# A decoder trunk's routing stage: PSUM operands for the choice of experts, three tiles chosen at once, and a new order of the first rows

## Chip, cores and metric

One core of one Trainium2 chip runs the whole kernel. The metric is device microseconds (us) of one execution; several executions are timed and the median is taken. Engines are named as in the profile: PE (matmuls), DVE, ACT, POOL, and SP, which issues the weight loads.

## What is computed

Two layers, 512 tokens of width 1024, everything in float32. Each layer is a mixer (attention of several kinds), an output projection with a layer norm, a router that sends every token to two of 16 experts, and the experts.

```python
x = layer_norm(ALPHA * x + mixer(x) @ w_o)             # "the output projection"
aff = sigmoid(x @ router_w)                            # 16 experts in 4 groups
sel = aff + router_bias
# group score: sum of the two highest sel of a group; the best group is kept,
# and in it the two highest experts; their aff, divided by their sum, are the gates
x = layer_norm(ALPHA * x + sum_e gate_e * (silu(x @ wg_e) * (x @ wu_e)) @ wd_e)
```

## The kernel before

**Tiles.** The residual `xr` lies in SBUF as four tiles of 128 tokens, two to a buffer (tiles 0 and 1 in "pair 0", tiles 2 and 3 in "pair 1"). A product in float32 is three matmuls (`mm3`): the operand is split into a high part (a cast on ACT, L185) and a low part (a subtraction on DVE, L186), and high by high, high by low and low by high are summed in PSUM (L198 to L200).

**Output projection and routing** (`out_proj`). For each tile and each half of 512 columns PE makes 12 matmuls, DVE adds the result to `xr` (L571) and takes statistics, PE transposes the sum (L576) and multiplies it by the router's weights (L580). With the statistics complete a Newton root on DVE gives the deviation, a sigmoid on ACT the affinities, ACT normalises the tile (L589), and `affine` applies the norm's gain and bias as two tensor operations, by POOL, for the last tile in part by DVE (L255, L256). Then POOL stores the tile twice to DRAM (`x1d`, L591, from which the experts' rows are gathered, and `yd`, L594, to which they are added). `choose` (L413 on) finds the two experts of each token, `slots` gives each token a slot of 96 in its expert, and `first_rows` (L490) multiplies `xr` by a one-hot matrix and so collects the first expert's rows without a gather. These three run for tiles 0 and 1, then tile 2, then tile 3 (`ROUTE_ORDER`).

**Experts** (`moe`). For every expert there are six loads of 1 MB: gate, up and down in two halves each, 96 a layer, all issued by SP in one order and each into a buffer of one of several kinds. The letter string `slot_of` gives the kind for each load in turn; "0" and "1" are the two pairs of `xr`, free as soon as their last reader, the stores among them, is done. The first 16 loads (`AHEAD`) are issued during the mixer and the output projection. `load` takes a ready one from a dictionary, and what isn't there it fetches:

```python
def load(w, e, c):
    if (w, e, c) in ahead:
        return ahead.pop((w, e, c))
    k = nload[0]
    nload[0] += 1
    return fetch(slot_of[k], w, e, c)
```

The order of PE for the first expert is: the gate's product ("g0", eight blocks k0 to k7 of three matmuls, two blocks to a half of a load), the up product ("u0"), the transposes of the next expert's rows (`rows_in(1)`, L1111), then the gate's product of expert 1 ("g1"). `put_rows` copies the first rows from PSUM as high and low part (L203, L204). `after_slots` (L493 to L529) makes one-hot matrices of the slots on DVE and multiplies them on PE, once into the token index of each slot (`idx`, L507, by which POOL gathers the rows of experts 1, 2 and so on, L1100), once into the gate of each slot (`gslot`). It is written before the first expert; the scheduler of the framework places its small matmuls between those of g0. The scheduler orders each engine's instructions by the order in the program and by what is ready in its own estimate; `tc.issue_after(x)` forces what is written inside it to stand behind `x` on the same engine.

Of the kernel before, what the change touches and what calls it, by code (L numbers as in the profile page):

```python
# [54 lines left out]
ROUTE_ORDER = "y0 l0 y1 l1 y2 l2 y3 l3 r02 r23 r34"  # L55
# [12 lines left out]
def trunk_kernel(ctx: ExitStack, tc, x_in, even_w_in, even_b_f, even_sinks, odd_w_in,  # L68
# [92 lines left out]
    hold = [None]  # L161
    in_order = [False]
# [25 lines left out]

    def ksplit(w, n, eng=V):
# [5 lines left out]
        return rows  # L195

    def mm3(o, lh, ll, rh, rl, first, last):
        T.matmul(o, lh, rh, start=first, stop=False)  # L198
        T.matmul(o, lh, rl, start=False, stop=False)  # L199
        T.matmul(o, ll, rh, start=False, stop=last)  # L200

    def split_to(hdst, ldst, src):
        first(A.copy(hdst, src))  # L203
        first(V.tensor_tensor(out=ldst, in0=src, in1=hdst.bitcast(F32), op=ALU.subtract))  # L204

    def rsqrt(var, eps, n, pin=lambda ins: ins):
# [20 lines left out]
        c = square(q, v)  # L227
        pin(V.scalar_tensor_tensor(out=p, in0=c, scalar=-10.0 / 3, in1=c, op0=ALU.add, op1=ALU.mult))
# [184 lines left out]
    def choose(t0, t1):  # L413

        n = t1 - t0
        ts_ = slice(t0, t1)
        sel = sm.tile([128, NT, NE], F32, name="sel", bufs=1)[:, 0:n]
        V.tensor_tensor(out=sel, in0=aff[:, ts_], in1=rb.unsqueeze(1).to_broadcast([128, n, NE]), op=ALU.add)
        sg = sel.rearrange("p t (g j) -> p (t g) j", j=4)
# [3 lines left out]
        V.tensor_tensor(out=pr[:, :, 2:4], in0=sg[:, :, 0:4:2], in1=sg[:, :, 1:4:2], op=ALU.add)  # L423
        V.tensor_tensor(out=pr[:, :, 4:5], in0=sg[:, :, 0:1], in1=sg[:, :, 3:4], op=ALU.add)
        V.tensor_tensor(out=pr[:, :, 5:6], in0=sg[:, :, 1:2], in1=sg[:, :, 2:3], op=ALU.add)
        gs = sm.tile([128, NT, 4], F32, name="gs")[:, 0:n]
        V.tensor_reduce(out=gs.rearrange("p t g -> p (t g)"), in_=pr, axis=AX.X, op=ALU.max)
# [22 lines left out]
        f8 = sm.tile([128, NT, 2], F32, name="rf8")[:, 0:n]  # L450
# [3 lines left out]
        V.tensor_tensor(out=M[:, ts_], in0=O[:, ts_, 0, :], in1=O[:, ts_, 1, :], op=ALU.add)  # L454
# [12 lines left out]
    def slots(sl, oh0, t0, t1):  # L467
# [5 lines left out]
        for j in range(1, t1):  # L473
# [5 lines left out]
        return V.tensor_tensor(out=oh0[:, t0:t1], in0=slot1.unsqueeze(1).to_broadcast([128, n, CAP]),  # L479
                               in1=sl[:, t0:t1, 0:1].to_broadcast([128, n, CAP]), op=ALU.is_equal)  # L480

    def first_rows(ps2, oh0, t0, t1):

        for c in range(2):
# [8 lines left out]
    def after_slots(sl, oht, flag):  # L493

        Of = O.rearrange("p t c e -> p (t c) e")
        R = sm.tile([128, NT * 2, NE], F16, name="R", bufs=1)
        V.tensor_tensor(out=R, in0=Of, in1=recc.rearrange("p t c -> p (t c)").unsqueeze(2).to_broadcast([128, 8, NE]), op=ALU.mult)
# [3 lines left out]
        V.tensor_reduce(out=pos, in_=t.rearrange("p t c e -> p (t c) e"), axis=AX.X, op=ALU.add)  # L501
        sp = ps_s()
        for j in range(NT * 2):
            oh = sm.tile([128, CAP], F16, name="oh", bufs=4)
            V.tensor_scalar(oh, slot1, pos[:, j:j + 1], None, op0=ALU.is_equal)
            T.matmul(sp[:CAP, 0:NE], oh, R[:, j, :], start=(j == 0), stop=(j == NT * 2 - 1))
        V.tensor_scalar(idx[:CAP], sp[:CAP, 0:NE], OOB, None, op0=ALU.add)  # L507
# [11 lines left out]
        weights()  # L519

        og = sm.tile([128, NT * 2, NE], F32, name="og", tag="gt", bufs=1)
        V.tensor_tensor(out=og, in0=O.rearrange("p t c e -> p (t c) e"),
                        in1=gates.rearrange("p t c -> p (t c)").unsqueeze(2).to_broadcast([128, 8, NE]), op=ALU.mult)
        sg = ps_t()
        for j in range(NT * 2):
            eq = sm.tile([128, CAP], F32, name="eq")
            V.tensor_scalar(eq, slot1, pos[:, j:j + 1], None, op0=ALU.is_equal)
            T.matmul(sg[:CAP, 0:NE], eq, og[:, j, :], start=(j == 0), stop=(j == NT * 2 - 1))
        A.activation(out=gslot[:CAP], in_=sg[:CAP, 0:NE], func=AF.Copy, scale=1.0 / ALPHA)  # L529

    def half_proj(chunk, oH, oL, g, i):
        o = ps_a()
        for k in range(4):
            ts_ = slice(i * 128, (i + 1) * 128)
            mm3(o, oH[4 * g + k][:, ts_], oL[4 * g + k][:, ts_], *chunk[k], k == 0, k == 3)
        return o

    def out_proj0(chunk_src, oH, oL, g, cs=range(2)):

        for c in cs:  # L540
            rows = ksplit(wload(chunk_src(c, g), 4, 512), 2, G)
            for i in range(NT):
                ys = xr[i][:, c * 512:(c + 1) * 512]
                V.scalar_tensor_tensor(out=ys, in0=ys, scalar=ALPHA, in1=half_proj(rows, oH, oL, g, i),
                                       op0=ALU.mult, op1=ALU.add)

    def out_proj(l, chunk_src, oH, oL, g, x1d, yd, work, main):
# [5 lines left out]
        sts = [sm.tile([128, 2, 6], F32, name="st", tag="st", bufs=4) for _ in range(NT)]  # L553
        if main:
            rwg, rsc = router_fold(l)
            u = sm.tile([128, NT, NE], F32, name="u", bufs=1)
            lgs = ps_s()[:, 0:2 * NT * NE].rearrange("p (c t e) -> p c t e", c=2, t=NT)
# [3 lines left out]
            work.tile([128, 4, CAP], F32R, name="hH", tag="hH")  # L561
            work.tile([128, 4, CAP], F32R, name="hL", tag="hL")
# [4 lines left out]

        def tile_y(i):
            for c in range(2):
                ys = xr[i][:, c * 512:(c + 1) * 512]  # L570
                V.tensor_tensor(out=ys, in0=ys, in1=half_proj(rows[c], oH, oL, g, i), op=ALU.add)  # L571
                V.bn_stats(sts[i][:, c, :], ys)
                if main:
# [3 lines left out]
                    yT = work.tile([128, 512], F32, name="yT", tag="sg", bufs=2)  # L577
                    A.copy(yT, p)
                    for k in range(4):
                        T.matmul(lgs[:, c, i, :], yT[:, k * 128:(k + 1) * 128], rwg[:, c * 4 + k, :],  # L580
                                 start=(k == 0), stop=(k == 3))

        def tile_ln(i):
            mv, rs = ln_stats(sts[i:i + 1])
# [822 lines left out]
```

## Time and profile before

| what | value |
|---|---|
| time, median of 3 runs | 1175.6 us (1171.33 to 1185.86) |
| the profiled execution | 1180.26 us, of which 1178.5 us are the span of the trace |
| PE busy | 1093.0 us, 93% of the span |
| DVE busy | 934.3 us, 79% |
| ACT busy | 762.3 us, 65% |
| POOL busy | 266.5 us, 23% |
| moved by DMA | 262.25 MB, mean 223 GB/s |

"Busy" is the time in which an engine has an instruction in execution. The profile's granted clock of TensorE is a share of 2.4 GHz: 1.00 is that, 0.50 is 1.2 GHz. A share of DMA near 1 says that the 16 DMA engines always had packets in flight. The routing stage of the first layer lies at some 220 to 288 us of the span, that of the second at 790 to 875 us.

### The profile page before, as it was taken

How to read it: one execution, taken by the hardware profiler on the slowest of the kernel's cores; microseconds unless marked ns; L12 is line 12 of the kernel's file. 1: busy time of each engine (PE TensorE's matmuls, PEld its weight loads, DVE VectorE, ACT ScalarE, POOL GpSimd, SP SyncE). 2: the span in 40 equal slices, each digit the busy share in tenths (PEclk: the TensorE clock that was granted, in tenths of full speed). 3: DMA queues.
4: the chain of work that ended last, by engine and by line, in shares of the span. 5: the costliest groups of instructions: out<-in, count | busy, mean ns of one | idle time of the engine just before them, and what ended most of it. 6: DMA issues, size and time to landing. Idle time of an engine off the chain costs nothing. (4 is left out here: it accounts for less than half of the span.)

```text
span 1178.5 us, 16701 instructions
## 1 busy us (share of the span) xinstructions
PE 1093.0 (93%) x5775; PEld 817.5 (69%) x5775; DVE 934.3 (79%) x1866; ACT 762.3 (65%) x1229; POOL 266.5 (23%) x223
## 2 busy tenths in 40 slices
PE   8999989979999999998599898999799999999982
PEld 7786767867777777776377665777677777777761
DVE  4646756597999999987766998766879999999976
ACT  4556646235888888887435744654268888888862
POOL 2001340251111141112613133003411111411023
PEclk9999999988999999999699998999789999999997
DMA  8314332779999997998512211335699999989972
GB/s 209 117 40 90 75 88 105 255 276 303 302 358 357 350 334 237 361 357 279 183 28 72 73 37 37 107 108 209 240 299 285 365 342 353 339 255 366 371 234 108
DMA packets 139613, 262.25 MB, mean 223 GB/s; under 512 B 11831, under 2 KB 28247, under 8 KB 139520
## 3 DMA queue, kind: packets, MB, share of 16 engines
q1 hardware_dynamic: 129232, 234.62, 57.9%
q0 software_dynamic: 10288, 26.48, 9.1%
q8 instruction: 47, 0.77, 0.3%
q14 instruction: 46, 0.38, 0.1%
HBM read 246.73 MB, written 22.30 MB: 228 GB/s over the span
## 5 line engine op out<-in xcount | busy, mean ns | idle before, releaser
L186 DVE TENSOR_TENSOR wl<-wraw,wh 128x1024 fp32r<-128x1024 f32 (+1 forms) x418 | 503.6, 1231 | 83.3 <-ACT wh L185 74.9
L185 ACT CAST wh<-wraw 128x1024 fp32r<-128x1024 f32 (+3 forms) x436 | 445.7, 1039 | 155.0 <-PE ps_s L200 63.8
L198 PE MATMUL ps_s<-wh,m 128*96 128x512 f32 (+1 forms) x528 | 208.3, 394 | 1.7 <-ACT m L203 1.7
L199 PE MATMUL ps_s<-wl,m 128*96 128x512 f32 (+1 forms) x528 | 206.4, 391 | 0.0
L200 PE MATMUL ps_s<-wh,m 128*96 128x512 f32 (+1 forms) x528 | 205.0, 388 | 0.4 <-DVE m L204 0.4
L200 PEld LDWEIGHTS ps_s<-wh,m 128*96 128x96 f32 x528 | 86.4, 164 | 35.7 <-DVE m L204 1.3
L198 PEld LDWEIGHTS ps_s<-wh,m 128*96 128x96 f32 x528 | 86.7, 164 | 34.8 <-ACT m L203 2.1
L199 PEld LDWEIGHTS ps_s<-wl,m 128*96 128x96 f32 x528 | 86.4, 164 | 31.9 <-issue 0.2
L198 PE MATMUL ps_a<-wh,hH 128*96 128x512 f32 x256 | 102.7, 401 | 3.8 <-ACT hH L203 3.8
L199 PE MATMUL ps_a<-wl,hH 128*96 128x512 f32 x256 | 101.8, 398 | 4.0 <-POOL wl L186 4.0
L200 PE MATMUL ps_a<-wh,hL 128*96 128x512 f32 x256 | 101.0, 394 | 1.3 <-DVE hL L204 1.3
L198 PE MATMUL ps_a<-wh,XH 128*128 128x512 f32 (+2 forms) x224 | 89.4, 399 | 4.3 <-ACT wh L185 3.2
L1100 POOL DMA_INDIRECT m<-x1d,idx x30 | 33.1, 1104 | 255.8 <-PE ps_t L1111 224.2
L200 PE MATMUL ps_a<-wh,XL 128*128 128x512 f32 (+2 forms) x224 | 88.7, 396 | 1.9 <-DVE XL L204 1.9
L1175 POOL DMA_INDIRECT yd<-m,idx x30 | 49.2, 1640 | 177.0 <-ACT m L1174 173.3
L199 PE MATMUL ps_a<-wl,XH 128*128 128x512 f32 (+2 forms) x224 | 88.8, 396 | 0.0
L199 PE MATMUL ps_a<-XL,wh 128*128 128x512 f32 x160 | 65.0, 406 | 0.0
L200 PE MATMUL ps_a<-XH,wl 128*128 128x512 f32 x160 | 64.7, 405 | 0.3 <-DVE wl L186 0.3
L198 PE MATMUL ps_a<-XH,wh 128*128 128x512 f32 x160 | 64.6, 403 | 0.0
L357 ACT ACTIVATE p<-p,nm 128x256 f32<-128x256 f32 (+3 forms) x96 | 50.6, 529 | 17.8 <-DVE nm L350 8.8
L376 ACT COPY pT<-ps_t 128x512 f32<-128x512 f32 (+2 forms) x88 | 43.4, 517 | 28.8 <-PE ps_t L373 28.0
L199 PEld LDWEIGHTS ps_a<-wl,hH 128*96 128x96 f32 x256 | 41.3, 161 | 20.5 <-POOL wl L186 5.4
(327 smaller groups left out, 1918.3 us busy)
## 6 DMA issues: line engine op xcount, KB each, us to landing
wraw<-in_moe_w_up_dram SPq DMA_DIRECT2D x64, 1024.0 KB
wraw<-in_moe_w_gate_dram SPq DMA_DIRECT2D x64, 1024.0 KB
wraw<-in_moe_w_down_dram SPq DMA_DIRECT2D x64, 1024.0 KB
wraw<-in_w_o_dram SPq DMA_DIRECT2D x6, 1024.0 KB
wraw<-in_even_w_in_dram SPq DMA_DIRECT2D x4, 1024.0 KB
x1d<-xr POOLq DMA_DIRECT2D x8, 512.0 KB
yd<-xr POOLq DMA_DIRECT2D x8, 512.0 KB
xr<-yd SPq DMA_DIRECT2D x8, 512.0 KB
```

The costliest lines, as they stand in the source:

```text
L185: first(A.copy(hv, w))
L186: first(eng.tensor_tensor(out=lv, in0=w, in1=hv.bitcast(F32), op=ALU.subtract))
L198: T.matmul(o, lh, rh, start=first, stop=False)
L199: T.matmul(o, lh, rl, start=False, stop=False)
L200: T.matmul(o, ll, rh, start=False, stop=last)
L357: A.activation(out=pt[h], in_=(pt if bias else Sp)[h], func=AF.Exp, bias=nm[:, h:h + 1], scale=(slopes[0][h] if slopes else 1.0), accum_ou ...
L376: A.copy(d_, s_)
L1100: G.indirect_dma_start(out=xg_of[e], out_offset=None, in_=x1d[:, :], in_offset=bass.IndirectOffsetOnAxis(ap=idx[:CAP, e:e + 1], axis=0), b ...
L1175: G.indirect_dma_start(out=yd[:, :], out_offset=bass.IndirectOffsetOnAxis(ap=idx[:CAP, e:e + 1], axis=0), in_=yos[e % 2], in_offset=None, ...
```

## The change

**The choice.** The sigmoid is written twice, to `aff` in SBUF and to spare columns of the PSUM bank that holds the router's logits; in `choose` each operation with two tensors takes one of them from PSUM. The root for one tile uses operations with two scalars from memory in place of a second tensor. Tiles 0, 1 and 2 are chosen at once, then tile 3.

**The norm.** The variance of tiles 0 and 1 comes from a Square on ACT. The affine of tiles 0 to 2 is all on POOL; tile 3's is done in four steps on DVE (`centre` and `whole`, each for two halves).

**The first rows.** The last tile's steps, the first rows' parts and g0's low parts follow each other in a written order (`in_turn`). The token index is made between k5 and k6 of g0 (`between`), the gates of the slots after u0, and what is needed only at the layer's end in expert 4.

**The first gate's weights.** g0's four halves of loads are cut by a comprehension that calls `load` once per half.

```diff
-AHEAD = (2, 3, 4, 0, 1, 5, 6, 8, 9, 10, 12, 13, 7, 14, 11, 15)
-LN1_DVE = (0, 0, 0, 256)
+AHEAD = (2, 3, 4, 0, 1, 5, 6, 8, 9, 10, 12, 13, 14, 11, 15, 7)
-ROUTE_ORDER = "y0 l0 y1 l1 y2 l2 y3 l3 r02 r23 r34"
+ROUTE_ORDER = "y0 l0 y1 l1 y2 l2 c03 y3 s03 l3 r03"
...
-    def choose(t0, t1):
+    def choose(t0, t1, sc):
+        affp, selp, gp, f8 = (t[:, ts_] for t in sc)
-        V.tensor_tensor(out=sel, in0=aff[:, ts_], in1=rb.unsqueeze(1).to_broadcast([128, n, NE]), op=ALU.add)
+        for t in (selp, sel):
+            V.tensor_tensor(out=t, in0=affp, in1=rb.unsqueeze(1).to_broadcast([128, n, NE]), op=ALU.add)
-        V.tensor_tensor(out=pr[:, :, 0:2], in0=sg[:, :, 0:2], in1=sg[:, :, 2:4], op=ALU.add)
+        V.tensor_tensor(out=pr[:, :, 0:2], in0=sg[:, :, 0:2], in1=sp[:, :, 2:4], op=ALU.add)
...
+        def centre(h):
+            return V.scalar_tensor_tensor(out=ys, in0=ys, scalar=end["mu"], in1=gb[:, cs], op0=ALU.subtract, op1=ALU.mult)
+        def whole(h):
+            return V.scalar_tensor_tensor(out=ys, in0=ys, scalar=end["rs"], in1=bb[:, cs], op0=ALU.mult, op1=ALU.add)
...
-        g0 = [ksplit(load("g", 0, c), 2) for c in range(2)]
-        for c in range(2):
-            put_rows(c, ps2[c])
-        after_slots(sl, oht, flag)
-        for e in (1, 2):
-            gather(e)
+        with tc.issue_after(route["act"].ins):
+            raws = [load("g", 0, c)[:, u * 2:u * 2 + 2, :] for c in range(2) for u in range(2)]
+            units = []
+            for w in raws:
+                with tc.issue_after(units[-1][2].ins) if units else nullcontext():
+                    units.append(high(w))
+        in_turn(lambda: route["whole"](0))
+        route["rows"](0)
+        low_part(0)
+        in_turn(lambda: route["whole"](1))
+        route["rows"](1)
+        route["x1"]()
+        in_turn(lambda: put_rows(0, ps2[0]))
+        low_part(1)
+        in_turn(lambda: put_rows(1, ps2[1]))
+        low_part(2)
+        def between():
+            with tc.issue_after(last_mm[0].ins):
+                in_turn(lambda: found.extend(slot_tokens(sl, route["room"])) or found[0])
+            low_part(3)
+            for i in (1, 2):
+                gather(i)
...
         for e in range(NE):
-            g = up("g", e, None if e else g0)
+            g = up("g", e, *((None,) if e else (g0, 1, between)))
+            if e == 4:
+                with tc.issue_after(act_op[0].ins):
+                    for_the_end(sl, oht, flag)
...
             sg = act(g, u, n)
+            if e == 0:
+                with tc.issue_after(put.ins):
+                    slot_weights(found[1])
```

The order of SP's loads around the end of the first layer's output projection, before (the first two rows are the last ahead loads, `wraw50` and `wraw52` are the two pairs of `xr`, and the two loads into them are the gate halves of expert 3):

```order
L1092 DMA wraw4_2822<-in_moe_w_gate_dram 128x4x512 [waits DMAHW0_49]
L1092 DMA wraw_2824<-in_moe_w_down_dram 128x4x512 [waits DMASW5_49,DMASW4_49,DMAHW1_49,DVE_49,Pool_49]
L1092 DMA wraw50_3346<-in_moe_w_gate_dram 128x4x512 [waits DMASW4_49,DMASW5_49,DMASW3_49,DMAHW2_49,DMASW2_49,PE_49]
L1092 DMA wraw52_3368<-in_moe_w_gate_dram 128x4x512 [waits DMASW6_49,DMASW1_49,DMASW7_49,DMASW0_49,DMAHW3_49,PE_49,Activation_49]
L1092 DMA wraw4_3400<-in_moe_w_up_dram 128x4x512 [waits DMAHW4_49,DVE_49]
```

The same place of SP now:

```order
L1196 DMA wraw4_2781<-in_moe_w_gate_dram 128x4x512 [waits DMAHW7_49,DMASW2_49]
L1196 DMA wraw50_2789<-in_moe_w_gate_dram 128x4x512 [waits DMASW3_49,DMASW4_49,DMASW2_49,DMASW5_49,DVE_49,DMAHW0_49,PE_49,Pool_49]
L1196 DMA wraw_2783<-in_moe_w_down_dram 128x4x512 [waits DMAHW1_49,DVE_49,Pool_49]
L1196 DMA wraw50_3662<-in_moe_w_gate_dram 128x4x512 [waits DMAHW2_49,DMAHW0_49,DVE_49]
L1196 DMA wraw3_2785<-in_moe_w_up_dram 128x4x512 [waits DMAHW3_49,DVE_49,Activation_49]
L1196 DMA wraw52_2791<-in_moe_w_gate_dram 128x4x512 [waits DMASW6_49,DMASW7_49,DMASW1_49,DMAHW4_49,DMASW0_49,PE_49]
L1196 DMA wraw52_3684<-in_moe_w_gate_dram 128x4x512 [waits DMAHW5_49,DMAHW4_49,DVE_49]
L1196 DMA wraw4_3310<-in_moe_w_gate_dram 128x4x512 [waits DMAHW6_49,DVE_49]
```

Two more gate loads stand in the row (272 weight loads in the whole program where there were 268), `wraw50_2789` and `wraw52_2791`, both into the pairs of `xr`, both behind waits on stores (DMASW) and on PE. In the second layer the two stand directly one after the other, behind the second down half.

DVE at the first rows of the first layer, now (`wl` is a low part, `m2` the first rows, `xr2` the pair of tiles 2 and 3; L680 is `whole`):

```order
L680 SCALAR_TENSOR_TENSOR xr2_130<-xr2_130,rs_o_2682,lnt_2296 128x512 [waits DMASW3_49]
L195 TENSOR_TENSOR wl_2794<-wraw3_2761,wh_2793 128x1024 [waits DMAHW5_49,Activation_49]
L680 SCALAR_TENSOR_TENSOR xr2_130<-xr2_130,rs_o_2682,lnt_2296 128x512
L214 TENSOR_TENSOR m2_2788<-ps_o_2345,m2_2788 128x384 [waits Activation_49]
L195 TENSOR_TENSOR wl_2797<-wraw50_2789,wh_2796 128x1024 [waits DMAHW0_49,Activation_49]
L214 TENSOR_TENSOR m2_2788<-ps_s_2346,m2_2788 128x384 [waits Activation_49]
L195 TENSOR_TENSOR wl_2800<-wraw3_2763,wh_2799 128x1024 [waits DMAHW6_49]
...
L537 TENSOR_SCALAR idx_135<-ps_s_2849 96x16 [waits PE_49]
L195 TENSOR_TENSOR wl_2803<-wraw52_2791,wh_2802 128x1024 [waits DMAHW4_49,Activation_49]
L186 TENSOR_TENSOR wl_2879<-wraw4_2755,wh_2878 128x1024 [waits DMAHW2_49,Activation_49]
```

The low parts of g0 come from four buffers: the two ahead loads (`wraw3_2761`, `wraw3_2763`) and the two new loads. Before, they came from the two ahead loads alone, and were made before the first rows were there.

PE at the end of u0 in the first layer, now (L546 are the gates of the slots, L1215 the transposes of expert 1's rows, the last row begins g1):

```order
L209 MATMUL ps_s_2877<-wl_2903,m2_2788 96x512
L210 MATMUL ps_s_2877<-wh_2902,m2_2788 96x512
L546 MATMUL ps_t_2931<-og_2929,yT_2850 96x16 [waits DVE_49]
L546 MATMUL ps_t_2931<-og_2929,yT_2850 96x16 x3
L546 MATMUL ps_t_2931<-og_2929,yT_2856 96x16 x4
L1215 MATMUL ps_t_2941<-ident_77,m1_2787 128x96 [waits DMASW2_49]
L1215 MATMUL ps_t_2941<-ident_77,m1_2787 128x96 x3
L1215 MATMUL ps_t_2948<-ident_77,m1_2787 128x96 [waits Activation_49]
L1215 MATMUL ps_t_2948<-ident_77,m1_2787 128x96 x3
L208 MATMUL ps_s_3000<-wh_3001,m2_2788 96x512 [waits Activation_49]
```

And DVE's row up to the `og` that L546 waits for:

```order
L186 TENSOR_TENSOR wl_3002<-wraw4_2759,wh_3001 128x1024 [waits Activation_49]
L488 TENSOR_TENSOR as__2925<-a2_2923 128x4 [waits DVE_49]
L186 TENSOR_TENSOR wl_3006<-wraw4_2759,wh_3005 128x1024 [waits Activation_49]
L489 RECIPROCAL as__2925<-as__2925 128x4 [waits DVE_49]
L186 TENSOR_TENSOR wl_3022<-wraw2_2765,wh_3021 128x1024 [waits DMAHW7_49,Activation_49]
L490 TENSOR_TENSOR gates_134<-a2_2923,as__2925 128x8 [waits DVE_49]
L186 TENSOR_TENSOR wl_3026<-wraw2_2765,wh_3025 128x1024 [waits Activation_49]
L542 TENSOR_TENSOR og_2929<-O_132,gates_134 128x128 [waits DVE_49]
```

The gates' matmuls moved from between those of g0 and u0 to behind u0, and their operand `og` stands on DVE behind the four low parts of g1.

## Rows read from the trace of the kernel before

**Rows 1.** Busy time of each engine in a stretch of the experts: PE, PEld, DVE, ACT, POOL, clock, DMA, GB/s.
```profile
300.00:320.00 20.00, 20.00 (x99) 14.30 (x98) 18.64 (x21) 17.16 (x22) 3.62 (x3) 1.00 0.97 320
```

**Rows 2.** DVE in order of time, first layer; columns: start, duration, engine, line, operation.
```profile
234.30 0.69 DVE L571 TENSOR_TENSOR xr<-xr,ps_a 128x512 f32<-128x512 f32 x1 [0.52 <-PE ps_a L200]
235.64 1.74 DVE L418 TENSOR_TENSOR sel<-aff,rb 128x32 f32<-128x32 f32 x1
237.51 2.40 DVE L423 TENSOR_TENSOR pr<-sel 128x16 f32<-128x16 f32 x1
...
247.97 0.67 DVE L571 TENSOR_TENSOR xr<-xr,ps_a 128x512 f32<-128x512 f32 x1
252.18 0.69 DVE L571 TENSOR_TENSOR xr<-xr,ps_a 128x512 f32<-128x512 f32 x1 [0.48 <-PE ps_s L475]
```

**Rows 3.** POOL in order of time, beside rows 2.
```profile
234.94 2.39 POOL L255 TENSOR_TENSOR xr<-xr,lnt 128x1024 f32<-128x1024 f32 x1 [1.80 <-ACT xr L589]
237.41 2.46 POOL L256 TENSOR_TENSOR xr<-xr,lnt 128x1024 f32<-128x1024 f32 x1
```

**Rows 4.** DVE, first layer: choosing for tile 3, its first and its last operation.
```profile
263.80 0.16 DVE L418 TENSOR_TENSOR sel<-aff,rb 128x16 f32<-128x16 f32 x1
266.42 0.17 DVE L454 TENSOR_TENSOR M<-O 128x16 f16<-128x16 f16 x1
```

**Rows 5.** PE, first layer: transposes that waited for an add, and two matmuls soon after.
```profile
242.58 0.66 PE L576 MATMUL ps_t<-ident,xr 128*128 128x128 f32 x4 [2.90 <-DVE xr L571]
...
247.27 0.63 PE L200 MATMUL ps_a<-wh,XL 128*128 128x512 f32 x1
247.70 0.63 PE L198 MATMUL ps_a<-wh,XH 128*128 128x512 f32 x1
```

**Rows 6.** Busy time of each engine in three windows of the routing stages, columns as in rows 1.
```profile
245.00:250.00 5.00, 5.00 (x16) 4.23 (x17) 3.49 (x7) 2.29 (x3) 1.87 (x1) 0.50 0.13 52
270.00:275.00 5.00, 5.00 (x27) 4.25 (x27) 2.25 (x9) 1.62 (x4) 0.00 (x0) 0.61 0.92 363
...
855.00:860.00 5.00, 4.38 (x28) 4.31 (x25) 2.79 (x14) 0.96 (x2) 0.00 (x0) 0.50 0.91 328
```

**Rows 7.** DVE, second layer: the fifth of the eight adds.
```profile
819.47 0.69 DVE L571 TENSOR_TENSOR xr<-xr,ps_a 128x512 f32<-128x512 f32 x1 [0.52 <-PE ps_a L200]
```

**Rows 8.** PE: the first matmul of g0 and the transposes behind u0, both layers.
```profile
272.57 0.77 PE L198 MATMUL ps_s<-wh,m 128*96 128x512 f32 x1
285.97 0.82 PE L1111 MATMUL ps_t<-ident,m 96*128 96x96 f32 x8
...
859.64 0.77 PE L198 MATMUL ps_s<-wh,m 128*96 128x512 f32 x1
873.18 0.82 PE L1111 MATMUL ps_t<-ident,m 96*128 96x96 f32 x8
```

**Rows 9.** POOL: the first of tile 3's two stores, both layers.
```profile
264.06 0.59 POOL L591 DMA_DIRECT2D x1d<-xr  x1 [0.30 <-POOL xr L256]
851.33 0.59 POOL L591 DMA_DIRECT2D x1d<-xr  x1 [0.82 <-DVE eq L512]
```

**Rows 10.** SP: the two loads into the pairs of `xr` as one group, both layers.
```profile
264.39 10.54 SPq L1092 DMA_DIRECT2D wraw<-in_moe_w_gate_dram  x2
851.46 11.74 SPq L1092 DMA_DIRECT2D wraw<-in_moe_w_gate_dram  x2
```

**Rows 11.** ACT and DVE, first layer: a high and a low part of a weight.
```profile
274.91 1.05 ACT L185 CAST wh<-wraw 128x1024 fp32r<-128x1024 f32 x1 [1.38 <-DMA wraw<-in_moe_w_gate_dram]
276.24 1.22 DVE L186 TENSOR_TENSOR wl<-wraw,wh 128x1024 fp32r<-128x1024 f32 x1
```

**Rows 12.** PE, g0 in the second layer: two matmuls that follow each other without a gap.
```profile
868.16 0.40 PE L199 MATMUL ps_s<-wl,m 128*96 128x512 f32 x1
868.40 0.39 PE L200 MATMUL ps_s<-wh,m 128*96 128x512 f32 x1
```

**Rows 13.** PE, first layer: four of the eight matmuls that make the gates of the slots.
```profile
276.54 0.43 PE L528 MATMUL ps_t<-og,eq 128*96 128x16 f32 x4
```

More of the change, by code (lines that the diff above doesn't have):

```diff
@@ L187, in unit, with high, low @@
         return h, l
+    def high(w):
+        h, l = (hl.tile([128, 1024], F32R, name="w" + t.lower(), tag=t).rearrange("p (a b) -> p a b", a=2) for t in "HL")
+        return h, l, A.copy(h, w)
+    def low(w, h, l):
+        return V.tensor_tensor(out=l, in0=w, in1=h.bitcast(F32), op=ALU.subtract)
     def ksplit(w, n, eng=V):
@@ L453, in choose @@
                         in1=f8.rearrange("p t c -> p (t c)").unsqueeze(2).to_broadcast([128, 2 * n, NE]), op=ALU.is_equal)
-        V.tensor_tensor(out=M[:, ts_], in0=O[:, ts_, 0, :], in1=O[:, ts_, 1, :], op=ALU.add)
+        with nc.allow_low_precision("ones and zeros"):
+            return V.tensor_reduce(out=M[:, ts_], in_=O[:, ts_].rearrange("p t c e -> p t e c"), axis=AX.X, op=ALU.add)
     def weights():
@@ L518, in after_slots, with half_proj @@
         V.tensor_reduce(out=flag, in_=cnt[:, 0:NE], axis=AX.X, op=ALU.max)
[L519 to L531, printed above, removed]
+    def half_proj(chunk, oH, oL, g, i, behind=None):
         o = ps_a()
@@ L534, in half_proj @@
             ts_ = slice(i * 128, (i + 1) * 128)
-            mm3(o, oH[4 * g + k][:, ts_], oL[4 * g + k][:, ts_], *chunk[k], k == 0, k == 3)
+            with tc.issue_after(behind.ins) if behind and k else nullcontext():
+                mm3(o, oH[4 * g + k][:, ts_], oL[4 * g + k][:, ts_], *chunk[k], k == 0, k == 3)
         return o
@@ L566, in out_proj, with room, by_act @@
         rows = [ksplit(wload(chunk_src(c, g), 4, 512), 2) for c in range(2)]
+        def room():
+            return work.tile([128, 512], F32, name="yT", tag="sg", bufs=2)
+        def by_act(i):
+            return main and i < 2
+        sts = [sm.tile([128, 2, 6], F32, name="st", tag="st", bufs=4) for _ in range(NT)]
         def tile_y(i):
@@ L583, in tile_ln @@
+        end = {}
         def tile_ln(i):
-            mv, rs = ln_stats(sts[i:i + 1])
+            if by_act(i):
+                V.tensor_scalar(ls[:, i, 2:3], ls[:, i, 1:2], -1.0 / (D * 32), None, op0=ALU.mult)
+                A.activation(out=sq, in_=xr[i], func=AF.Square, bias=ls[:, i, 2:3], scale=1.0 / 32,
+                             accum_out=ls[:, i, 4:5])
+                rs = rsqrt(ls[:, i, 4:5], LN_EPS, 1)
+            else:
+                mv, rs = ln_stats(sts[i:i + 1])
             if main:
@@ new lines, in tile_ln @@
+                A.activation(out=sc[0][:, i, :], in_=u[:, i, :], func=AF.Sigmoid)
+                end["act"] = A.activation(out=aff[:, i, :], in_=u[:, i, :], func=AF.Sigmoid)
+            if i == NT - 1 or not main:
+                end.update(mu=mv[:, 0, 0:1], rs=rs)
+                return
+            nm = sm.tile([128, 1], F32, name="nmr", bufs=4)
+            if by_act(i):
+                V.tensor_scalar(nm, ls[:, i, 2:3], 32.0, rs, op0=ALU.mult, op1=ALU.mult)
+            else:
+                V.tensor_scalar(nm, mv[:, 0, 0:1], -1.0, rs, op0=ALU.mult, op1=ALU.mult)
@@ L591, in tile_ln, with x1 @@
+            with tc.issue_after(end["act"].ins):
+                A.activation(out=xr[i], in_=xr[i], func=AF.Identity, scale=rs, bias=nm)
+            affine(xr[i], gb, bb, 0)
+            x1(i)
+        def x1(i):
             nc.gpsimd.dma_start(x1d[i * 128:(i + 1) * 128, :], xr[i])
```

187 lines of the change are left out of this document (124 added, 63 removed).

## Prediction

> **What bounds the kernel now.** I read the busy shares first, then the windows, then each engine in order of time in the two routing stages. Inside the experts PE has no gap: 20.00 of 20 us busy at a clock of 1.00 [rows 1], so nothing that the change does there can help, and each matmul added there costs its time. It touches the stages between the output projection and the second expert, where PE waits and then runs slowly. The reader sees it in [rows 5]: the transposes of the sixth add wait 2.90 us, and the matmuls after them follow each other by 0.43 us (247.27 to 247.70), against 0.24 us at full clock [rows 12]. The clock is 0.50 in 245 to 250 and 855 to 860 and 0.61 in 270 to 275 [rows 6], that is at or near 1.2 GHz instead of 2.4. A wait of some 3 us is paid twice, then: as idle time, and in slow matmuls for some 5 us after it.
>
> The wait comes from DVE: adding the router's bias takes 1.74 us and one addition of pairs 2.40 us [rows 2], where the same bias addition takes 0.16 in [rows 4]. Each of the two ends with a POOL affine that began before it or with it (234.94 and 2.39, 237.41 and 2.46) [rows 3]. Both slow operations read two tensors from SBUF; the add of the projection, which reads one from PSUM, takes its usual 0.69 beside the first affine [rows 2].
>
> **Sum, part 1: up to the first matmul of g0.** With one operand in PSUM I take those two operations at 0.16 each, so 3.8 us go. Undisturbed adds follow each other by 4.2 us (247.97 to 252.18) [rows 2]. From the fifth add at 234.30 the seventh then comes at 242.7 instead of 247.97; in the second layer, from 819.47 [rows 7], at 827.9. Call it t. The added operations are short: sigmoid and bias are written twice (four instructions a layer at some 0.2), and choosing three tiles adds six searches at some 0.2, while one call of 2.8 us [rows 4] goes.
>
> What is late next is the eighth add: it stands on DVE behind the choice of tiles 0 to 2. Statistics, root and sigmoid of the third tile are about 3.4 us (an estimate: 0.7 like the add, twelve short operations at 0.2, the sigmoid), the choice of three tiles 4.5 (2.8 for one tile [rows 4] and the longer searches), with a gap 8.4 us instead of 4.2: t+8.4. PE idles some 3 us there, and the clock falls again, as after the 2.90 us of [rows 5]. Then tile 3: transposes, logits and root at half clock 4.6, sigmoid 0.4, first `centre` and choice 3.4, second `centre`, slots and one-hot 1.1, `whole` 0.7 (0.69 for 512 columns [rows 2]), a low part 1.2 [rows 11], `whole` 0.7: t+20.5. The stores of tile 3 are issued at about t+20.6 = 263.3 and 848.5, against 264.06 and 851.33 [rows 9], and g0's first matmul runs at about t+21 = 264 and 849, against 272.57 and 859.64 [rows 8]. That is 8.6 and 10.6 us gained at this point. Most of it is the low parts and the token index that no longer stand ahead of g0.
>
> **Part 2: the weights of g0.** The gain isn't kept, and this is the core of the forecast. The comprehension calls `load` for g0's first half, which pops the ahead load, and then again for the same half, which is no longer in the dictionary: so it is fetched a second time, into the pairs of `xr`. The order shows both: two gate loads more a layer, and their low parts in g0's row. Blocks k2 and k3 use the first reload, k6 and k7 the second. The first goes into pair 0, whose tiles were stored long before. The second goes into pair 1 and needs tile 3's two stores landed. Before, the load into that pair stood under the same condition but was for expert 3, and nobody waited for it. How long it takes is in [rows 10]: SP's group of two ends at 274.93 and 863.20, so with about 0.5 us for the issue the second went out at 274.4 and 862.7, 10.4 and 11.4 us after the store's issue [rows 9], while loads shared the DMA.
>
> First layer: 263.3 + 10.4 = 273.7. Then the reload must land. Alone, 1.05 MB at 363 GB/s (270 to 275 in [rows 6]) are 2.9 us; with the two MB issued just ahead of it 8.7. I take 6.8: 280.5. High and low part are 1.05 and 1.22 [rows 11], so k6 starts at 282.8. Blocks k0 to k5 are over by some 274, so PE has idled long and starts at half clock: of the 30 matmuls left to the end of u0, 14 at 0.43 and 16 at 0.24 are 9.8 us: 292.6, against 285.97 [rows 8], **+6.6 us**.
>
> Second layer: 848.5 + 11.4 = 859.9, here both reloads stand ahead of the next loads, 5 us: 864.9; k6 at 867.2, u0 ends at 877.0, against 873.18 [rows 8]: **+3.8 us**. Bounds of this part: with the reload landing 2.9 us after its issue, 3.9 and 2.1 us less; with all the two MB ahead in the way, and the stores delayed by the 2.9 us of one more MB, 4.8 and 6 more.
>
> **Part 3: gates of the slots behind u0.** L546 waits for `og`, which DVE makes behind the four low parts of u0 and the four of g1: 8 x 1.22 and five short operations, 10.8 us after k6 can start. PE needs 9.8, so it waits 1.0; the eight matmuls take 0.87 (0.43 for four [rows 13]). They were made before too, but in slack. **+1.9 us** a layer. Were PE at full clock there, u0 would end 2.8 us earlier and the wait be 3.7 at most. Behind the waiting matmuls stand the transposes of expert 1's rows and g1; both wait with them.
>
> **Part 4: smaller ones.** With two loads more the count passes the ahead loads at once, so all gathers are queued in expert 0, and the rows of expert 3 may reach their place on PE before their gather: nothing to 3 us a layer; I take 1. The end's matmuls, now in expert 4 where PE is full [rows 1], **+0.7 us** a layer (eight small matmuls at 0.1 as in [rows 13]); before, they were in a gap. The two MB more a layer cost the stream nothing as long as PE waits for something else; if the loads behind them come late, 2.1 MB at 363 GB/s are 5.8 us a layer. The Square on ACT, the affine on POOL alone: both engines have room beside PE's work there. I take zero; 1 us either way.
>
> **The sum.** 6.6 + 3.8 + 2 x 1.9 + 2 x 1 + 2 x 0.7 = 17.6 us on the profiled execution's 1180.26, 1197.9. That execution is 4.7 us over the median of the runs shown, so I forecast **1193 us**, 1.5% longer: all that is gained ahead of g0 is lost in it. A measurement of this kernel tells about 2% from no change (23.5 us), so this counts as within.
>
> **A rule against part 2.** The wait for the stores is 10.4 and 11.4 us in [rows 9, 10]. The Trainium skill, "DMA: Bandwidth & Descriptors", section "Anatomy of one DMA — SWDGE (gpsimd) path", gives a fixed 2.0 us and then the bytes at 436 GB/s for one transfer. By it the two stores would be done 4.4 us after their issue and a reload 4.4 us after that; an estimate from that page alone puts the whole at about 1177. The rows are for shared engines and speak against it here; what a quick landing would do is rival 1.
>
> **Rivals.**
> 1. *The reload comes in time.* If stores and reload land quickly (nothing queued ahead of them), k6 follows k5. From 264 and 849, 48 matmuls, 20 of them at 0.43, take 15.3 us: u0 ends at 279.3 and 864.3, 6.7 and 8.9 us earlier than before. With 3.7 a layer for part 3 and 3.4 for part 4 the sum is -4.8: 1171, not slower. For it: the first reload is issued early, and DMA has a pause, 52 GB/s in 245 to 250 [rows 6]. Against it: [rows 10], and the windows at 328 and 363 GB/s [rows 6].
> 2. *Later still, slower by over 2%.* The stores and reloads take 2.9 us longer in each layer, because each has one MB more beside it: +5.8. And the wait for `og` becomes 2.8 us or more, after which g1's 24 matmuls run by 0.43 instead of 0.24, +4.6 in one of the layers. Together 1203. It decides from a landing of the second reload at about 283 in the first layer. For it: a wait of 2.90 us did drop the clock in [rows 5, 6]. Against it: PE comes out of a longer wait there already, and is itself late for `og`.
> 3. *The PSUM operands don't free DVE.* Then t stays at 247.97 and stores and reload move by some 4 us a layer: 1201. Against it: the 0.69 of the add beside POOL [rows 2, 3].
>
> **Chances.** Forecast 0.47, rival 1 0.18, rival 2 0.25, rival 3 0.10. Range 1170 to 1209: from rival 1 to rival 2 with the later bound of part 2. Faster by over 2% (below 1152) would need rival 1 and no cost in parts 3 and 4 and more: 0.05. Slower by over 2% (above 1199): most of rivals 2 and 3 and the upper edge of the forecast, 0.35. Within: 0.60.
>
> **What would show it.** In the trace after: the bias and pair additions at 0.2 or less beside POOL; the stores of tile 3 near 263 and 848; first g0 matmul near 264 and 849; then a PE wait of some 8 us before the seventh block, its releaser ACT or DVE on the part of a gate load; the clock at 0.50 behind it; the transposes of expert 1 at about 294 and 879. Wrong: no PE wait inside g0, or SP issuing the second reload less than 6 us after the stores.

## The result: 4.95% slower

The changed kernel takes 1238.14 us (median of 4 runs, 1235.9 to 1241.5), the kernel before beside it 1180.61: a ratio of 1.0495, interval 1.0448 to 1.0543. The forecast was 1193 with a range to 1209. Its direction was right, its size wrong by a factor of about three: 57.5 us instead of 17.6.

The profile after has a span of 1234.1 us. First DVE in order of time in the first layer, beside [rows 2]:

```profile
245.22 0.69 DVE L624 TENSOR_TENSOR xr<-xr,ps_a 128x512 f32<-128x512 f32 x1 [1.57 <-PE ps_a L210]
249.57 0.22 DVE L443 TENSOR_TENSOR ps_s<-ps_s,rb 128x48 f32<-128x48 f32 x1 [0.31 <-ACT ps_s L651]
251.14 0.18 DVE L464 TENSOR_TENSOR ps_s<-ps_s,desc 128x12 f32<-128x12 f32 x1
253.00 0.25 DVE L476 TENSOR_TENSOR O<-io,ps_s 128x96 f16<-128x96 f32 x1
259.32 0.69 DVE L624 TENSOR_TENSOR xr<-xr,ps_a 128x512 f32<-128x512 f32 x1 [5.79 <-PE ps_a L210]
```

The bias addition that took 1.74 us takes 0.22, and nothing in the choice is long any more. That addition is no proof for the PSUM operands, though, for POOL has no affine in execution at 249.57. The operation at 251.14 is beside one, and takes 0.18:

```profile
250.88 2.33 POOL L272 TENSOR_TENSOR xr<-xr,lnt 128x1024 f32<-128x1024 f32 x1 [1.80 <-ACT xr L662]
```

But between the seventh add (245.22) and the eighth (259.32) lie 14.1 us, and DVE is idle for 5.79 of them. It waits for PE. PE in order of time, the rows that waited long or that answer to [rows 8], first and then second layer:

```profile
253.40 1.86 PE L633 MATMUL ps_s<-rwgb,yT 128*128 128x16 f32 x8 [4.99 <-DVE O L476]
272.30 0.47 PE L208 MATMUL ps_s<-wh,m 128*96 128x512 f32 x1 [0.57 <-ACT m L213]
294.26 0.74 PE L208 MATMUL ps_s<-wh,m 128*96 128x512 f32 x1 [12.98 <-ACT wh L192]
307.07 2.74 PE L546 MATMUL ps_t<-og,yT 128*96 128x16 f32 x16 [2.60 <-DVE og L542]
350.12 1.51 PE L1215 MATMUL ps_t<-ident,m 96*128 96x96 f32 x8 [5.10 <-DMA m<-x1d,idx]
...
869.50 1.86 PE L633 MATMUL ps_s<-rwgb,yT 128*128 128x16 f32 x8 [4.99 <-DVE O L476]
887.19 0.62 PE L208 MATMUL ps_s<-wh,m 128*96 128x512 f32 x1 [0.57 <-ACT m L213]
900.10 0.74 PE L208 MATMUL ps_s<-wh,m 128*96 128x512 f32 x1 [8.81 <-ACT wh L192]
905.38 1.45 PE L535 MATMUL ps_s<-R,yT 128*96 128x16 f32 x16
908.23 0.47 PE L209 MATMUL ps_s<-wl,m 128*96 128x512 f32 x1 [0.87 <-DVE wl L195]
918.25 2.74 PE L546 MATMUL ps_t<-og,yT 128*96 128x16 f32 x16 [3.29 <-DVE og L542]
959.16 1.19 PE L1215 MATMUL ps_t<-ident,m 96*128 96x96 f32 x6 [3.03 <-DMA m<-x1d,idx]
```

There are four long waits in each layer. The router's logits wait 4.99 us for DVE's choice. Then g0 begins, at 272.30 where the forecast had 264 and the kernel before 272.57. Inside g0 PE waits 12.98 and 8.81 us for the cast of a reload, but not of the same one: in the first layer it is block k6 that waits, for the second reload. In the second layer it is k2, for the first reload; the token index (L535), which stands between k5 and k6, comes only behind it, and k6 then waits 0.87. The gates of the slots wait 2.60 and 3.29. Expert 3's rows wait 5.10 and 3.03 for their gather. After each the clock is low; the windows after three of them in the first layer, columns as in [rows 1]:

```profile
250.00:255.00 5.00, 1.60 (x8) 1.63 (x8) 3.16 (x24) 0.80 (x1) 4.04 (x2) 0.50 0.35 136
295.00:300.00 5.00, 4.80 (x12) 3.24 (x12) 4.88 (x6) 3.10 (x4) 0.00 (x0) 0.50 0.61 227
310.00:315.00 5.00, 5.00 (x19) 3.49 (x18) 1.12 (x2) 1.98 (x4) 0.95 (x1) 0.61 0.53 188
```

The second reload in the first layer: POOL issues tile 3's stores, SP the reload, and what SP queues next waits for it (groups of SP's waits: total, times, longest).

```profile
272.64 0.53 POOL L667 DMA_DIRECT2D x1d<-xr  x1 [15.57 <-DVE xr L680]
```
```profile
278.40 0.37 SPq L1196 DMA_DIRECT2D wraw<-in_moe_w_up_dram  x1
281.61 0.37 SPq L1196 DMA_DIRECT2D wraw<-in_moe_w_gate_dram  x1
```
```profile
SPq L1196 <- DMA wraw<-in_moe_w_gate_dram: 12.6, 2, 11.2
```

From the stores to the issue of the reload are 9.0 us (272.64 to 281.61), from its issue to the release of the next load 11.2. The first reload in the second layer, SP in order of time, the group of SP's waits that stands ahead of it, then ACT:

```profile
887.31 0.37 SPq L1196 DMA_DIRECT2D wraw<-in_moe_w_down_dram  x1
887.90 0.37 SPq L1196 DMA_DIRECT2D wraw<-in_moe_w_gate_dram  x1
```
```profile
SPq L1196 <- DVE xr L680: 11.2, 1, 11.2
```
```profile
899.00 1.99 ACT L192 CAST wh<-wraw 128x1024 fp32r<-128x1024 f32 x2 [8.60 <-DMA wraw<-in_moe_w_gate_dram]
```

It stands on SP behind the second down half, which waits 11.2 us for DVE's last `whole` (L680). So it goes out at 887.90, and its cast begins 11.1 us later.

Of the 57.5 us, some 33 are there at the first layer's transposes of expert 3's rows (350.12 against 317.3 before), and 55 by those of the second layer (959.16 against 904.5).

### The profile page after: what moved, and what is told of

The parts are those of the page before. It is cut to its first block, busy times and chain, and to the rows that moved or that the text cites. A ratio compares the mean times of both kernels' runs of the same rounds, so it can differ in the third digit from the quotient of the medians.

```text
span 1234.1 us, 16668 instructions
## 1 busy us (share of the span) xinstructions
PE 1106.8 (90%) x5787; PEld 821.3 (67%) x5787; DVE 916.8 (74%) x1818; ACT 765.6 (62%) x1243; POOL 268.7 (22%) x219
## 4 chain that ended last, share of the span: by engine, by line
PE 60%; DVE 13%; DMA 11%; issue 9%; ACT 5%; POOL 2%; SPq 0%; POOLq 0%; DVEq 0%; ACTq 0%
PE ps_a L210 9%; PE ps_a L208 9%; PE ps_a L209 9%; PE ps_s L209 6%; PE ps_s L210 6%; PE ps_s L208 6%; DMA wraw<-in_moe_w_down_dram 5%; PE ps_o L397 3%; PE ps_t L390 3%; DMA m<-x1d,idx 3%; DVE wl L186 2%; ACT wh L185 2%; DMA wraw<-in_odd_w_in_dram 2%; DMA wraw<-in_moe_w_gate_dram 1%; PE ps_t L1215 1%
## 5 line engine op out<-in xcount | busy, mean ns | idle before, releaser
L186 DVE TENSOR_TENSOR wl<-wraw,wh 128x1024 fp32r<-128x1024 f32 (+1 forms) x410 | 492.2, 1228 | 93.8 <-ACT wh L185 86.1
L185 ACT CAST wh<-wraw 128x1024 fp32r<-128x1024 f32 (+3 forms) x428 | 437.1, 1038 | 158.6 <-PE ps_s L210 58.7
L208 PE MATMUL ps_s<-wh,m 128*96 128x512 f32 (+1 forms) x528 | 210.0, 398 | 23.1 <-ACT wh L192 21.8
L210 PE MATMUL ps_s<-wh,m 128*96 128x512 f32 (+1 forms) x528 | 208.2, 394 | 0.0
L1283 POOL DMA_INDIRECT yd<-m,idx x30 | 57.8, 1927 | 282.4 <-ACT m L1282 274.4
L208 PE MATMUL ps_a<-wh,h 128*96 128x512 f32 x256 | 104.0, 406 | 3.9 <-ACT h L213 3.9
L209 PE MATMUL ps_a<-wl,h 128*96 128x512 f32 x256 | 102.5, 400 | 5.4 <-DVE wl L186 2.9
L210 PE MATMUL ps_a<-wh,h 128*96 128x512 f32 x256 | 103.2, 403 | 1.3 <-DVE h L214 1.3
L1204 POOL DMA_INDIRECT m<-x1d,idx x30 | 44.0, 1465 | 171.7 <-PE ps_t L1215 122.3
L209 PEld LDWEIGHTS ps_a<-wl,h 128*96 128x96 f32 x256 | 42.3, 165 | 24.7 <-DVE wl L186 4.6
```

Of the source, the lines that this page charges most:

```text
L185: first(A.copy(hv, w))
L186: first(eng.tensor_tensor(out=lv, in0=w, in1=hv.bitcast(F32), op=ALU.subtract))
L210: last_mm[0] = T.matmul(o, ll, rh, start=False, stop=last)
L1204: G.indirect_dma_start(out=xg_of[e], out_offset=None, in_=x1d[:, :], in_offset=bass.IndirectOffsetOnAxis(ap=idx[:CAP, e:e + 1], axis=0), b ...
L1283: G.indirect_dma_start(out=yd[:, :], out_offset=bass.IndirectOffsetOnAxis(ap=idx[:CAP, e:e + 1], axis=0), in_=yos[e % 2], in_offset=None, ...
```

## Experiments

All ten kernels compute the same as the changed kernel. Each ratio is to runs of the kernel before on the same chip.

| run | time, us | ratio, interval |
|---|---|---|
| the change | 1238.14 | 1.0495 (1.0448 to 1.0543) |
| one load (e1) | 1198.91 | 1.0152 (1.0101 to 1.0204) |
| one load, own bank (e2) | 1202.11 | 1.0164 (1.0108 to 1.0220) |
| one load, scratch in SBUF (e3) | 1195.96 | 1.0121 (1.0072 to 1.0170) |
| before, loads twice (e4) | 1220.77 | 1.0321 (1.0256 to 1.0385) |
| one load, free order (e5) | 1183.03 | 1.0032 (1.0003 to 1.0061) |
| one load, gates early (e6) | 1190.09 | 1.0076 (1.0041 to 1.0112) |
| one load, both (e7) | 1177.93 | 0.9968 (0.9941 to 0.9996) |
| the change, gathers late (e8) | 1223.45 | 1.0356 (1.0298 to 1.0414) |
| e7, slots first (e9) | 1172.17 | 0.9920 (0.9888 to 0.9951) |
| e9, end in the gap (e10) | 1172.57 | 0.9927 (0.9898 to 0.9957) |

**One load (e1).**

```diff
-            raws = [load("g", 0, c)[:, u * 2:u * 2 + 2, :] for c in range(2) for u in range(2)]
+            halves = [load("g", 0, c) for c in range(2)]
+            raws = [halves[c][:, u * 2:u * 2 + 2, :] for c in range(2) for u in range(2)]
```

> The changed kernel, but each half of g0's weights is loaded once and its two parts are cut from that one load: two loads of 1 MB less a layer, and the count of loads stays at the ahead loads, so the gathers are queued as before the change. Theory A (the second loads cost most of the time): the waits of 13.0 and 8.8 us before k6 go, with them some 5 us of slow matmuls after them, and the waits of 5.1 and 3.0 us for the rows of expert 3: 1186 to 1197 us instead of 1238. Rival B (the earlier wait, PE for the choice of tiles 0 to 2 at 5.0 us a layer, and the slow clock behind it are the main cost): 1215 us or more. Either way the first g0 matmul stays near 272 us in the first layer.

1198.91: 39 us come back, 2 us short of theory A's range, and 1.5% remain. PE now:

```profile
252.73 1.86 PE L633 MATMUL ps_s<-rwgb,yT 128*128 128x16 f32 x8 [4.99 <-DVE O L476]
271.58 0.47 PE L208 MATMUL ps_s<-wh,m 128*96 128x512 f32 x1 [0.57 <-ACT m L213]
281.59 0.48 PE L209 MATMUL ps_s<-wl,m 128*96 128x512 f32 x1 [1.39 <-DVE wl L195]
292.68 2.74 PE L546 MATMUL ps_t<-og,yT 128*96 128x16 f32 x16 [2.80 <-DVE og L542]
```

The 12.98 has become 1.39 and the wait for expert 3's rows is gone; the 4.99 and the wait for `og` stand.

**The kernel before with the second loads (e4).** Its g0 line is split in the same way, with a call of `load` for each part.

> The kernel before with only the second loads added: each half of g0's weights is loaded twice, nothing else differs. Theory A: the second reload waits for the stores of tile 3, k6 starts about 283 us, u0 ends 7 us later in the first layer and 5 in the second, and the gathers that are queued early cost up to 15 more together: 1195 to 1212, that is 15 to 32 us above the kernel before. Rival B: within 10 us of the kernel before, since its g0 starts at 272 and the reload has time.

+3.2%, or 38 us: more than expected, and nearly what e1 gives back. So the second loads alone explain two thirds of the loss, in either order of the rest. The extra has its rows: in the old order the first rows' cast (L203) stands on ACT behind the cast of the reload, so that g0's very first matmul waits. ACT, then PE:

```profile
281.04 1.04 ACT L185 CAST wh<-wraw 128x1024 fp32r<-128x1024 f32 x1 [5.58 <-DMA wraw<-in_moe_w_gate_dram]
281.99 0.47 ACT L203 CAST m<-ps_o 128x384 fp32r<-128x384 f32 x1
```
```profile
282.51 0.74 PE L198 MATMUL ps_s<-wh,m 128*96 128x512 f32 x1 [5.94 <-ACT m L203]
335.32 1.52 PE L1111 MATMUL ps_t<-ident,m 96*128 96x96 f32 x8 [5.71 <-DMA m<-x1d,idx]
```

**The change with the gathers queued as before (e8).**

```diff
-            if len(xgs) == 2 and nload[0] > len(AHEAD):
+            if len(xgs) == 2 and nload[0] > len(AHEAD) + 2:
```

> The changed kernel with its second loads, but the condition by which all gathers are queued in expert 0 is put back to where it was (two loads more before it holds). Theory D (the early queueing is a cost of its own: PE's waits of 5.1 and 3.0 us for the rows of expert 3 and the slow clock behind them): 12 to 16 us less than the changed kernel, 1222 to 1226. If those waits come from the second loads themselves (the DMA is late anyway): 1234 or more.

1223.45, as theory D says. PE's waits for the reloads stay (group of PE's waits in this run), those for expert 3's rows are gone:

```profile
PE ps_s L208 <- ACT wh L192: 22.9, 2, 12.8
```

So the second loads have two prices. The loads themselves cost 2.0 points (1.0356 to 1.0152, about 24 us); no run separates their landing late from the bytes that they add. The other 1.4 points, some 16 us, come from two loads more on a counter that a condition elsewhere reads: two more gather buffers are taken at once, in the memory of a load that is still to be used, and gather 3 waits for that. Its row in the changed kernel is on POOL:

```profile
341.61 1.99 POOL L1204 DMA_INDIRECT m<-x1d,idx  x1 [8.61 <-DVE wl L186]
```

**Scratch in banks of its own (e2).** The scratch columns go to the spare columns of the two banks that collect the first rows.

```diff
...
-            sc = scratch(bank[:, 2 * NT * NE:512])
+            ps2 = [ps_o(), ps_s()]
+            sc = scratch(ps2)
...
```

> As the run with one load, and the choice's scratch columns moved out of the bank of the router's logits, into the spare columns of the two banks that collect the first rows. Theory B (the matmuls of the logits wait for the choice because both are in one bank): PE's wait of 5.0 us for DVE's one-hot of experts goes in both layers, the eighth add comes some 5 us earlier, the first g0 matmul near 265: 10 to 16 us below the run with one load, so 1172 to 1185. If that wait isn't caused by the bank, the time is that of the run with one load.

1202.11, no gain. The 4.99 is gone, as theory B said: the logits now wait 1.41 us for DVE's `u`, and the eighth add comes at 255.03. But a wait of the same kind has come up where the scratch now lies. DVE's choice of tile 3 waits for the first rows' matmuls in other columns of that bank:

```profile
255.03 0.69 DVE L626 TENSOR_TENSOR xr<-xr,ps_a 128x512 f32<-128x512 f32 x1 [3.80 <-PE ps_a L210]
267.27 0.18 DVE L444 TENSOR_TENSOR ps_o<-ps_o,rb 128x16 f32<-128x16 f32 x1 [6.53 <-PE ps_o L517]
```

**Scratch in SBUF (e3).** This undoes the PSUM operands alone.

```diff
-            sc = scratch(bank[:, 2 * NT * NE:512])
+            sc = scratch(sm.tile([128, 152], F32, name="scr", bufs=1))
```

> As the run with one load, and the scratch of the choice in SBUF instead of PSUM, so that its operations read two operands from SBUF again. If DVE stalls beside POOL as before the change, the operations of the choice of three tiles show 1 to 2.4 us instead of 0.2, and the time is 0 to 8 us above the run with its own bank, though PE's logits no longer wait for the choice. If PSUM operands do nothing, DVE's choice takes the same time as with PSUM.

1195.96, by its interval not to be told from one load, nor from e2, above which it was expected. Both halves of the trade are in its rows, first DVE, then POOL:

```profile
248.35 0.17 DVE L463 TENSOR_TENSOR scr<-scr,gm 128x12 f32<-128x12 f32 x1
248.56 2.22 DVE L464 TENSOR_TENSOR scr<-scr,desc 128x12 f32<-128x12 f32 x1
```
```profile
248.39 2.37 POOL L272 TENSOR_TENSOR xr<-xr,lnt 128x1024 f32<-128x1024 f32 x1 [2.76 <-ACT xr L662]
```

The same operation with its operand in PSUM took 0.18 us beside POOL (251.14 in the changed kernel). In SBUF it takes 2.22, and another 2.20. But PE's logits don't wait for the choice, only 1.43 us for DVE's `u`. What the PSUM operands save, 4 us a layer, the bank takes back. The Trainium skill, "SBUF — State Buffer", section "Who interferes with whom", says that a DVE instruction with two inputs in SBUF contends with a POOL instruction that reads there and one with at most one such input doesn't; these rows agree.

**No written order for the last product (e5).** The edit drops the order for the second half of every tile, not of the last alone.

```diff
-                o = half_proj(rows[c], oH, oL, g, i, end.get("lg") if main and c else None)
+                o = half_proj(rows[c], oH, oL, g, i)
```

> As the run with one load (1199), without the written order that holds the projection's last product behind the logits of the half before it. The choice's scratch stays in the bank of the logits, so the logits still wait for the choice, but the product no longer stands behind them. Theory B: PE makes that product while DVE chooses, the eighth add comes some 5.7 us earlier in each layer (253 instead of 258.6 in the first), less is made at half clock: 8 to 14 us less than with one load alone, 1185 to 1191. If the order doesn't matter: 1196 to 1202.

1183.03, 16 us less than with one load, 2 more than expected. DVE's last two adds, then PE:

```profile
242.66 0.69 DVE L624 TENSOR_TENSOR xr<-xr,ps_a 128x512 f32<-128x512 f32 x1 [0.46 <-PE ps_a L210]
245.91 0.69 DVE L624 TENSOR_TENSOR xr<-xr,ps_a 128x512 f32<-128x512 f32 x1 [0.64 <-PE ps_a L210]
```
```profile
249.41 3.00 PE L633 MATMUL ps_s<-rwgb,yT 128*128 128x16 f32 x16 [2.10 <-DVE rs_r L241]
```

3.25 us apart, no longer 14.1, and g0 begins at 265.16 (of the 6.4 us to e1's 271.58, 2.9 lie ahead of the first add). The scratch is still in the bank of the logits, and PE still waits 2.10 us for DVE ahead of them, until the choice is near its end (the releaser that the profile names stands between the last two operations of the choice). So most of the harm came from the last product being forced to stand behind the matmuls that waited.

**Gates early (e6), and both (e7).** The DVE part of `slot_weights` is made right behind g0's last low part.

```diff
             low_part(3)
+            with tc.issue_after(put.ins):
+                found.append(slot_gates())
...
-                    slot_weights(found[1])
+                    slot_weights(found[1], found[2])
```

> As the run with one load, with the gates and their product with the one-hot made on DVE right behind g0's last low part; the matmuls of the gates stay behind u0. Theory C: the waits of 2.80 us a layer before them go, and with them the slow clock in which these matmuls (2.74 us) and the first of g1 run: 6 to 11 us less than with one load, 1188 to 1193. If DVE is what limits u0, the 1.2 us more on DVE ahead of it come back there: 1194 or more.

> Both edits on top of one load: no written order for the last product, and the gates early. If theories B and C are independent, the savings add up: 1174 to 1185, that is no more than the kernel before within 2%. If one wait only takes the place of the other, 1185 to 1191.

1190.09 and 1177.93: 9 us by itself, 5 on top of e5 (8 by the ratios). With DVE ahead of it PE runs the same matmuls at full clock, 1.45 us instead of 2.74. A shorter wait is left behind them, for ACT's copy of the gates, and g1 still starts at half clock; the run with gates early:

```profile
290.87 1.45 PE L549 MATMUL ps_t<-og,yT 128*96 128x16 f32 x16
294.15 0.90 PE L1218 MATMUL ps_t<-ident,m 96*128 96x96 f32 x4 [1.44 <-ACT gslot L550]
```

With both, the kernel is within a per cent of the one before.

**Slots first (e9), and the end in the gap (e10).** In e7 DVE waited for tile 3's slots, whose small matmuls stood behind 12 others (24 in the profile, which shows each of them as two):

```profile
265.74 0.17 DVE L502 SCALAR_TENSOR_TENSOR sl<-ps_s,M 128x16 f32<-128x16 f32 x1 [3.66 <-PE ps_s L500]
```

e9 takes the second half of the first rows for tiles 0 to 2 out of its place and puts it behind them:

```diff
...
+        with tc.issue_after(last_mm[0].ins):
+            first_rows(ps2, oh0, 0, n, (1,))
...
```

> As the run with both edits (1178), and the small matmuls of tile 3's slots stand before the second half of the first rows instead of behind it. In the run with both edits DVE waited 3.66 us for them. Theory: the last first rows and g0 come 1.5 to 3 us earlier in each layer: 1172 to 1176. If g0 is then bound by DVE's low parts: no change, 1177 to 1179.

> As the run with the slots first, and the matmuls that are needed only at the layer's end move from expert 4, where PE has no gap (rows come 18.4 instead of 17.7 us after the expert before), to the place where the token index is made. If PE waits there anyway (1.4 us): 0.7 us a layer less, 1.4 in all. If they delay the index and its gather: 0 to 2 us more than the run with the slots first.

1172.17, in the range: the wait is 0.99 us, and the kernel is the fastest so far, by 0.8% of the one before (e7 was ahead by 0.3%, with an interval that ends just under 1).

```profile
261.74 0.17 DVE L503 SCALAR_TENSOR_TENSOR sl<-ps_s,M 128x16 f32<-128x16 f32 x1 [0.99 <-PE ps_s L500]
```

Moving the end's matmuls gave 1172.57: the 1.4 us expected of it can't be told from nothing by these runs.

## Why the prediction was wrong

**Part 1 failed, in one step: "the eighth add: it stands on DVE behind the choice of tiles 0 to 2 ... t+8.4".** t was good: 245.22 against 242.7, with the routing stage itself beginning 3.4 us later than before (the first add at 221.12, against 217.68). It was good for another reason than the one given. In the new order no choice stands between the adds, and with the scratch in SBUF (e3) the seventh add comes 23.9 us after the first, with PSUM operands 24.1. DVE's choice was good too: the one-hot of experts is done at t+8.0. But I took the product for the eighth add as made by then. Three of its 12 matmuls were; the other nine hadn't begun. On PE they were held by a written order behind the logits of the half before, and those waited 4.99 us for the choice, because its scratch lies in their PSUM bank. Both were in the text of the changed kernel (`behind`, `scratch(bank[...])`), and I read neither as a wait. After that, the nine matmuls ran at half clock, 0.43 us apart. e2, e3 and e5 show the two halves of this: move the scratch and the wait moves, drop the order and the wait does less harm. Its price is 1.2 points, 14 to 16 us (e1 to e5). From the seventh add to g0's first matmul the forecast has 21.3 and 21.1 us, the trace 27.1 and 25.9. So of the 8.6 and 10.6 us that part 1 forecast as gained at g0's start, 3.7 and 5.8 are there, counted from the first add of each layer.

The Trainium skill has a rule that points at it: "PSUM — Partial Sum Buffer", section "PSUM bank collisions raise a hardware error", says that the compiler's scheduler adds a dependency between any two instructions on different engines that touch the same bank in the same 32 partitions, whatever the address. The 4.99 and the 6.53 us agree; I hadn't weighed it. This kernel's order is made by the scheduler of its framework, and in every run here what shares a bank also shares a tile of the program, so which of the two the wait is for stays open.

**Part 2 was right in the first layer, with one term mis-sized, and wrong on the load in the second.** The forecast had PE waiting 8.8 us at k6 in the first layer (274 to 282.8); 12.98 were measured. The wait for the stores was taken at 10.4 and was 9.0 us; the landing, taken at 6.8, was 11.2. In the second layer it had k6 late again, at 867.2, for the second reload. There k6 waited 0.87 us, and the 8.81 stand ahead of k2, for the first reload. The step that failed took the first reload as early in both layers ("The first goes into pair 0, whose tiles were stored long before"). The pair was free, but on SP the reload stood behind a load that waited 11.2 us for the last `whole`. That a wait of about the forecast size came all the same is luck. So is, in part, that the forecast and rival 1, the reload late or in time, are 22 us apart and e8 to e1 measured 24. The prediction had set a rule of the Trainium skill against this part ("DMA: Bandwidth & Descriptors", section "Anatomy of one DMA — SWDGE (gpsimd) path": 2.0 us and the bytes at 436 GB/s for one transfer that POOL issues). By estimate from it the two stores take 4.4 us; 9.0 passed here until the reload went out. The reload, issued by SP, isn't that section's case, and took 11.2. Three loads of 1 MB were issued in the 9.2 us ahead of the reload, and some 3 MB moved while it landed (281 GB/s in 281.6 to 292.8); that it waited its turn is inferred from this.

**Part 3 was mis-sized.** 1.9 us a layer were forecast. The wait was 2.60 and 3.29 instead of 1.0, and the eight matmuls took 2.74 instead of 0.87. The profile shows them as 16, so the four of [rows 13] are two of the eight, not four; and they ran at half clock (at full clock 1.45 in e6). e7 against e5 gives 0.6 points, 5 to 8 us for both layers, of which 3.8 had been counted.

**Part 4 was the second failed step: "the rows of expert 3 ... nothing to 3 us a layer; I take 1".** The waits were 5.10 and 3.03, and each drops the clock again (eight transposes take 1.51 us behind it, 0.82 in [rows 8]); e8 puts all of it at 1.4 points, 16 us instead of 2. The bound from above was itself too low: the first wait exceeds it, and it left out the slow matmuls after a wait, though the first paragraph of the forecast says that such a wait is paid twice. From expert 2's rows to expert 3's PE takes 26.2 and 24.1 us in the two layers, and 17.7 in e8: 15 us more, of which the waits are 8.1.

The sum, in points of the kernel before: gathers 1.4, reloads 2.0, written order 1.2, gates 0.6, together 5.3 against 4.95 measured; what the change saves otherwise is the remaining 0.3 (e7). These are steps from one run to the next, so they add up by construction, and each holds for the order in which they were undone; by their intervals each is good to some 0.4 to 0.8 points. The end's matmuls, 0.7 us a layer, are right by their rows: the rows of expert 5 come 18.4 us after those of expert 4, and 17.7 elsewhere. Rival 3 had no ground, since t doesn't hang on the PSUM operands (e3). Rival 2 had the right sign and too small a mechanism: its reload later by 2.9 us came true in the first layer (1.4 less for the stores, 4.4 more for the landing), but most of the excess came from ahead of the reload and from behind it.

What stays open: why the first layer's routing stage begins up to 4 us later in the runs of the new order (first transposes at 218.5 to 222.3, and 218.6 before) wasn't tried. e5 and e7, whose edits differ only behind this stage, are 3.8 us apart in it, so some of it may be a difference between executions.

## What to carry to other kernels

Before you count what a helper costs, look at what its calls do to shared state: here a comprehension that reads like slicing loaded 4 MB a second time, and moved a counter that a condition elsewhere depended on. Spare columns of a PSUM bank weren't free: DVE, which used them, waited for the matmuls of that bank and made them wait, and a written order then spread the wait to work that had nothing to do with it. And when a wait is bounded, bound the slow clock after it too, or the bound is no bound.

## What the runs showed of the hardware that was not expected

Matmuls and DVE operations in the same PSUM bank (and the same tile of the program), in columns that don't overlap, were kept apart by waits of 4.99 and 6.53 us; the wait followed the scratch from bank to bank (e2), and none of this kind was there with the scratch in SBUF (e3). A load of 1 MB took 11.2 us from issue to release when three loads were issued in the 9.2 us ahead of it and two gathers in the 2.2 us behind it, more than the stores that it had waited for.
